# The opening of a two layer encoder: order of the input loads, of the first operands and of the first weight sums

## The chip, the cores and the metric

The kernel runs on one core of a Trainium2 chip. The metric is device time in microseconds (us) of one execution; a lower time is better. Five engines work beside each other, each through its own queue: TensorE (PE, matmuls; PEld are its weight loads), VectorE (DVE), ScalarE (ACT), GpSimd (POOL) and SyncE (SP). DMA transfers are issued from the queues of SP, ACT and POOL. All arithmetic is on float32 data; for matmuls each operand is split into a rounded part and a remainder, as told below.

## The reference

The program is a trunk of two macaron layers over 512 tokens plus 16 learned meta tokens, 528 in all, of width 1024. Each layer is a half-weighted SwiGLU block, a mixer of two parallel branches (gated linear attention and grouped-query softmax attention), and another half-weighted SwiGLU block:

```python
def swiglu(x, w_gate, w_up, w_down):
    return (jax.nn.silu(x @ w_gate) * (x @ w_up)) @ w_down

def reference(x, meta_tokens, norm_gains, ...):
    h = jnp.concatenate([meta, x], axis=1)
    for l in range(DEPTH):
        h = h + 0.5 * swiglu(rmsnorm(h, norm_gains[l, 0]), ffn_w_gate[l, 0], ffn_w_up[l, 0], ffn_w_down[l, 0])
        h = h + mixer(rmsnorm(h, norm_gains[l, 1]), ...)
        h = h + 0.5 * swiglu(rmsnorm(h, norm_gains[l, 2]), ffn_w_gate[l, 1], ffn_w_up[l, 1], ffn_w_down[l, 1])
    return rmsnorm(h, final_norm)[:, N_META:]
```

Only the first SwiGLU block of layer 0 is touched by the change: `rmsnorm`, then `x @ w_gate` and `x @ w_up` with an inner width of 2816.

## The kernel before

**Layout.** The tokens lie along the free dimension. `h` (`hall`) is one tile of 128 partitions x 8 chunks x 528 tokens; chunk c holds features 128c to 128c+127. `halves` are the token ranges 0:264 and 264:528, `HF` is 264.

**Two parts for each operand.** A value is used as `hi`, its copy rounded to the matmul type by ACT, and `lo`, value minus `hi`, by DVE. A product is three matmuls: hi x hi, hi x lo, lo x hi. For weights the two parts are made by `Weights.make` (cast on line 290 into `whi`, difference on line 291 into `wlo`), for 128x1024 at a time, in four buffers each.

**Seven products in place of eight.** The gate and up products of the SwiGLU block take the two by two block scheme with seven products (Strassen's, in a form with chained sums). The activations' blocks are two chunks (a pair j of chunks 2j and 2j+1) by two token halves: b11, b12 are the halves of the first chunk, b21, b22 those of the second. The weights' blocks 11, 12, 21, 22 are stored as 128x1024 pieces in `win`. Products are named "1" to "7". Each is 24 matmuls of 128x264: four chunk pairs k, gate and up (j), three combinations of parts. Products 1, 2 and 4 use the weight blocks 11, 12 and 22 as they are (`DIRECT`). Products 7, 6, 5 and 3 use sums of blocks: s3 = 21 - 11, s2 = 22 + s3, s1 = 21 + 22, s4 = s2 - 12. The activations' side has seven blocks for each pair, in the order of `PLACE`: b11 (product 1), b21 (product 2), b12 - b11 (5), b22 minus that (6), b12 - b22 (7), b21 minus the block of product 6 (4), and -b22 (3). `Norm.pair` (line 508) makes all seven, in both parts, from two chunks scaled by the norm's gain (line 512): casts on lines 519 and 524, differences on 520, 525, 527, 528, 530 and 531.

**Columns of weights.** The 2816 inner columns are 11 pairs of 128-wide column blocks for gate and up, in groups of 4, 4 and 3. "P0-1" in what follows is product 1 of column pair 0. `ffn_steps(True)` gives the first block the order P0-1, P0-2, P1-1, P1-2, P0-4, P1-4, P0-6, P0-5, P0-7, P0-3, P1-6, P1-5, P2-1, P1-7, P2-2, P1-3, P2-6, and so on. `product_of_pair` (line 584) runs one product; its results are collected in PSUM tiles X, Y, Z and W and in SBUF tiles `c` (copies on lines 605 and 615, adds on line 611, 626, 627, 634). When a column pair is complete, `hidden` applies silu and the gate (lines 651, 447, 661).

**Sums of weights.** For column pairs 0 to 3 of the first block the sums are made by accumulating DMAs of POOL (`add`, line 209): ACT writes the negative of block 11 or 12 (line 204), POOL adds further blocks onto it out of DRAM or out of SBUF. `begin_sums` makes s3 and s2, `first_sum` makes s1, and `sums` calls them when the parts of a product's weights are made: in the first block's column pairs 0 and 1 (`OPENING`) `begin_sums` at product 1, `first_sum` and s4 at product 2. The tiles of s3 and s4 share three buffers (`long`), those of s2 and s1 another three (`short`). POOL's adds stand in one queue, so an add that waits holds up those behind it.

**Loads.** `fetch` issues the weights' loads on SP in the order of use, into three buffers (`raw`); a buffer is free again when the cast, the difference and, where there is one, the negative of it have run. `use` makes the parts three products ahead and fetches nine loads ahead.

**The norm.** The sum of squares (`Norm.square`, lines 502 and 506) is begun ahead of P0-5. A matmul with a constant matrix (line 474) gives the means, and ACT and DVE the reciprocal root (lines 480, 447, 485, 486, 558). It is needed only in `hidden`, since the norm's factor is applied behind the products. Line 768 scales the chunks of h with it; these are traced among the steps of column pairs 2 and 3.

**What sets the order.** The text is traced into instructions with dependencies, and a planner then orders each engine's queue by the order of the text and by which instruction it believes ready; an instruction whose inputs or buffer it believes not ready is passed by later ones. `issue_after` and `W.behind` pin an instruction behind another of the same engine. On the chip each queue then runs strictly in that order.

**The opening.** SP loads chunk 0, chunk 1, the first weights in two pieces, then chunks 2 to 7 in three loads. `first.pair(j)` alternates with `W.make`:

```python
    nc.sync.dma_start(h(1), xt[:, 1])
    first.pair(0)
    W.fetch(1)
    for c in (2, 4, 6):
        nc.sync.dma_start(hall[:, c : c + 2], xt[:, c : c + 2])
    W.make(1)
    W.fetch(2)
    first.pair(1)
```

Of the kernel before, what the change touches and what calls it, by code (L numbers as in the profile page):

```python
# [17 lines left out]
P = 128  # L18
# [153 lines left out]
class Weights:  # L172
# [41 lines left out]
    def begin_sums(self, f, i, w=None):  # L214

        got = self.summed
        s3 = None
        if self.chained(f, i):
            s3 = self.negative(f, i, "s3", w)
            self.add(s3, self.dram(f, i, "21"))  # L220
        elif i < NPAIR:
            s3 = self.block(f, i, "21", self.long, "wsa")
        s2 = self.block(f, i, "22", self.short, "wsb")
        if self.chained(f, i):
            self.add(s2, s3)
        got[f, i, "7"], got[f, i, "6"] = s3, s2
        if (f, i) not in OPENING:
            self.first_sum(f, i)

    def first_sum(self, f, i):  # L230
        s1 = self.block(f, i, "21", self.short, "wsb")
# [100 lines left out]
def build(tc, ctx, xt, wts, win, par, w2, const, umask, out):  # L332
# [32 lines left out]
    def nm(p):  # L365
        count[0] += 1
        return f"{p}{count[0]}"
# [22 lines left out]
    def h(c, cs=None):  # L390
        return hall[:, c, cs or slice(0, live[0])]
# [4 lines left out]
    nc.sync.dma_start(h(0), xt[:, 0])  # L396
    S.dma_start(pt, par)
    def load_constants():
        S.dma_start(ct[:, :C_O1024], const[:, :C_O1024])
# [88 lines left out]
    class Norm:  # L488


        def __init__(self, gc):
            self.gc, self.x, self.acc = gc, [], None

        def operand(self, c):
            hi, lo = slot("x", F32R), slot("x", F32R)
# [12 lines left out]
        def pair(self, j):  # L508
# [23 lines left out]
            parts(slice(4, 6), v2(t34))  # L532
            self.x.append((hi, lo))

        def chunk(self, c):
            self.operand(c)
            self.square(c)
# [35 lines left out]

    pending = [load_constants]

    def ffn(l, f, norm, done, following):

        x, rs, up, n = norm.x, None, None, live[0]
        w = n // 2
# [177 lines left out]
        for i, step in enumerate(steps):  # L757
# [26 lines left out]

    def project(x, rs, tag, f=1.0, n=T):
# [445 lines left out]
    def ending(sums, operand, rs):  # L1231
# [49 lines left out]
    nc.sync.dma_start(h(1), xt[:, 1])  # L1281
    first.pair(0)
# [6 lines left out]
    W.make(2)  # L1289
    W.fetch(3)  # L1290
    first.pair(2)
    W.make(3)
    W.fetch(4)
    first.pair(3)
    nc.sync.dma_start(ct[:, C_O1024 : C_O1024 + P], const[:, C_O1024 : C_O1024 + P])

    norms = [first] + [Norm(G_NORM + i * KC) for i in range(1, 3 * DEPTH)]
    for l in range(DEPTH):
        a, b, c = norms[3 * l : 3 * l + 3]
        ffn(l, 0, a, b.chunk, lambda: operand_pools(b, "x"))  # L1300
# [79 lines left out]
```

## Time and profile before

| | us |
|---|---|
| median of 3 runs (lowest, highest) | 2196.23 (2196.23, 2197.56) |
| the profiled execution's own time | 2196.04 |
| its span in the profile | 2194.3 |
| DVE busy | 1777.9 |
| ACT busy | 1215.5 |

In the profile "L601" is line 601 of the kernel, "out<-in" gives the tiles written and read, "x24" a count, and what stands in brackets is the idle time of the engine just before the instruction and what ended it. Times count from the start of the span. `ss<-xc,whi` is a matmul with the rounded weights, `ss<-xc,wlo` one with their remainder, `w<-win` a load of a weight block, or an add onto one, and `s` a tile of s3 or s4. The same bytes of DMA are read in both kernels: 16.78 MB in the first 60 us here.

### The profile page before, as it was taken

The numbers are of one execution on the slowest core, as the hardware profiler recorded it, in microseconds if no ns is written. First come the engines' busy times: TensorE is split into PE (matmuls) and PEld (weight loads), VectorE is DVE, ScalarE is ACT, GpSimd is POOL, SyncE is SP. The second block draws the span as 40 slices with busy tenths as digits, with TensorE's granted clock in tenths as the row PEclk, the third lists the DMA queues.
The fourth block names the chain that finished last, engine by engine and source line by source line (L and its number), as shares of the span: only waits on it lengthen the run. The fifth ranks groups of instructions, "written<-read, shape, count | busy, mean of one in ns | idle before, by whom it ended". The sixth has DMA issues, their size and how long they took to land.

```text
span 2194.3 us, 40087 instructions
## 1 busy us (share of the span) xinstructions
PE 2157.0 (98%) x16506; PEld 2066.7 (94%) x16506; DVE 1777.9 (81%) x2699; ACT 1215.5 (55%) x1781; POOL 105.3 (5%) x124
## 2 busy tenths in 40 slices
PE   7999999999999999999999999999999999999998
PEld 7999999989999999999999999999788888999997
DVE  7887977586976689788799879785878767997987
ACT  8545545354784556454575455453557836554543
POOL 1100000000000000010010000000000001000100
PEclk9999999999999999999999999999999999999999
DMA  9866743212113567676667667432121145776752
GB/s 282 218 194 184 200 125 111 78 49 68 49 39 120 129 176 182 202 182 184 165 164 186 198 181 203 127 109 80 49 78 49 49 134 151 197 202 181 195 161 68
DMA packets 87751, 312.46 MB, mean 142 GB/s; under 512 B 9744, under 2 KB 12176, under 8 KB 87568
## 3 DMA queue, kind: packets, MB, share of 16 engines
q1 hardware_dynamic: 68336, 244.48, 33.6%
q0 software_dynamic: 17280, 62.92, 16.1%
q10 hardware_dynamic: 1952, 2.50, 0.4%
q8 instruction: 130, 2.13, 0.4%
q14 instruction: 53, 0.43, 0.1%
HBM read 289.94 MB, written 2.10 MB: 133 GB/s over the span
## 4 chain that ended last, share of the span: by engine, by line
PE 76%; DVE 16%; ACT 4%; issue 2%; DMA 2%; SPq 0%; POOL 0%; DVEq 0%; ACTq 0%
PE ss L601 33%; PE mm L468 13%; PE ss L721 11%; PE ss L468 10%; DVE wlo L291 4%; PE sm L468 2%; DVE g L687 1%; PE sm L1083 1%; DVE c L683 1%; DVE g L683 1%; PE ss L1058 1%; DVE c L651 1%; DMA w<-win 1%; DVE g L661 1%; PE ss L474 1%
## 5 line engine op out<-in xcount | busy, mean ns | idle before, releaser
L601 PE MATMUL ss<-xc,whi 128*128 128x264 f32 (+1 forms) x4928 | 903.4, 285 | 11.6 <-ACT whi L290 7.4
L601 PEld LDWEIGHTS ss<-xc,whi 128*128 128x128 f32 x4928 | 764.8, 189 | 14.9 <-ACT whi L290 7.8
L601 PE MATMUL ss<-xc,wlo 128*128 128x264 f32 (+1 forms) x2464 | 700.7, 285 | 3.4 <-DVE wlo L291 3.3
L601 PEld LDWEIGHTS ss<-xc,wlo 128*128 128x128 f32 x2464 | 465.1, 189 | 5.2 <-DVE wlo L291 5.2
L291 DVE TENSOR_TENSOR wlo<-w,whi 128x1024 fp32r<-128x1024 f32 (+1 forms) x335 | 405.5, 1217 | 64.1 <-ACT whi L290 63.9
L290 ACT CAST whi<-w 128x1024 fp32r<-128x1024 f32 (+1 forms) x335 | 345.9, 1048 | 159.8 <-PE ss L601 80.3
L468 PE MATMUL mm<-x,whi 128*128 128x264 f32 (+1 forms) x1712 | 384.8, 315 | 0.0
L468 PEld LDWEIGHTS mm<-x,whi 128*128 128x128 f32 x1712 | 278.4, 188 | 16.6 <-issue 1.0
L468 PE MATMUL mm<-x,wlo 128*128 128x264 f32 (+1 forms) x856 | 266.1, 315 | 0.0
L721 PE MATMUL ss<-g,whi 128*128 128x264 f32 (+1 forms) x1280 | 237.0, 284 | 0.0
L290 ACT CAST whi<-raw 128x1024 fp32r<-128x1024 f32 x126 | 132.1, 1049 | 163.5 <-PE mm L468 102.7
L605 ACT COPY c<-ss 128x528 f32<-128x528 f32 (+1 forms) x132 | 78.5, 595 | 245.7 <-PE ss L601 245.3
L291 DVE TENSOR_TENSOR wlo<-raw,whi 128x1024 fp32r<-128x1024 f32 x126 | 153.9, 1222 | 59.3 <-ACT whi L290 58.4
L721 PEld LDWEIGHTS ss<-g,whi 128*128 128x128 f32 x1280 | 198.4, 188 | 0.1
L721 PE MATMUL ss<-g,wlo 128*128 128x264 f32 (+1 forms) x640 | 181.3, 283 | 0.0
L468 PEld LDWEIGHTS mm<-x,wlo 128*128 128x128 f32 x856 | 159.6, 188 | 8.5 <-issue 0.7
L468 PE MATMUL ss<-g,whi 128*128 128x264 f32 (+2 forms) x900 | 166.2, 299 | 0.0
L468 PEld LDWEIGHTS ss<-g,whi 128*128 128x128 f32 x900 | 131.7, 188 | 5.2
L209 POOL DMA_DIRECT2D w<-win x60 | 52.7, 879 | 1557.1 <-DVE t L1211 392.2
L721 PEld LDWEIGHTS ss<-g,wlo 128*128 128x128 f32 x640 | 120.5, 188 | 0.0
L447 ACT ACTIVATE c<-c 128x528 f32<-128x528 f32 (+1 forms) x88 | 56.5, 642 | 96.3 <-DVE c L651 96.1
L291 DVE TENSOR_TENSOR wlo<-s,whi 128x1024 fp32r<-128x1024 f32 x86 | 104.9, 1220 | 1.7 <-ACT whi L290 1.5
(268 smaller groups left out, 3374.0 us busy)
## 6 DMA issues: line engine op xcount, KB each, us to landing
w<-win SPq DMA_DIRECT2D x333, 512.0 KB, 4.5
raw<-wts SPq DMA_DIRECT2D x126, 512.0 KB, 3.3
w<-win POOLq DMA_DIRECT2D x60, 512.0 KB, 7.4
s<-win POOLq DMA_DIRECT2D x26, 512.0 KB, 7.6
w<-s POOLq DMA_DIRECT2D x26, 512.0 KB, 6.0
s<-w POOLq DMA_DIRECT2D x8, 512.0 KB, 8.0
h<-xt SPq DMA_DIRECT2D x3, 528.0 KB, 6.6
out<-h ACTq DMA_DIRECT2D x4, 256.0 KB, 2.4
```

Of the source, the lines that this page charges most:

```text
L209: self.nc.gpsimd.dma_start(t, src, accum_op=ALU.add)
L290: nc.scalar.copy(hi[:, cs], w[:, cs])
L291: nc.vector.tensor_tensor(lo[:, cs], w[:, cs], hi[:, cs].bitcast(F32), ALU.subtract)
L447: prev_act[0] = S.activation(*args, **kw).ins
L468: TE.matmul(acc.half[i][:width], lhs, rhs[:, acc.spans[i]], start=first, stop=last)
L474: TE.matmul(a, weights, x[:, hs], start=True, stop=True)
L601: TE.matmul(acc[:, j], a[:, j, k], b[:, at], start=bool(begin and k == 0 and i == 0), stop=k == len(x) - 1 and i == 2, skip_group_check=no ...
L605: W.behind = S.copy(part(st, q), acc).ins
L651: V.scalar_tensor_tensor(td, ts, -0.5, rs[:, cs], ALU.mult, ALU.mult)
L661: V.tensor_tensor(raw[p // 4][2 * m + q][:, p % 4], t[:, q * w : (q + 1) * w], us, ALU.mult)
L683: V.tensor_tensor(lo, src[:, ks], hi.bitcast(F32), ALU.subtract)
L721: TE.matmul(acc[:, j], a[:, j, k], xs[b][:, k], start=bool(begin and k == 0 and i == 0), stop=k == 3 and i == 2, skip_group_check=not begin)
```

## The change

The edits are all in the first block of layer 0.

1. The loads of x go by token halves: first halves of chunks 0 and 1, P0-1's weights, first halves of chunks 2 and 3, then of 4 to 7, the weights of P0-2 and P1-1, then the second halves.
2. `Norm.pair` isn't used for this block. `head` makes the operands of products 1 and 2 (b11 and b21) straight from `h`, for all four pairs, ahead of the products. `fourth` scales whole chunks and makes the operand of product 4, `middle` those of 5 and 6, `rest` those of 7 and 3. They are called between the steps of `ffn`: `fourth` for pairs 0 and 1 behind P0-1, for 2 and 3 behind P0-2, `middle` for all behind P1-2, `rest` behind P0-4.
3. For column pairs 0 and 1 the negatives are written at products 1 and 2 as before; the loads and adds of the sums (`open_sums`) stand behind P0-2 for pair 0 and behind P1-2 for pair 1.
4. `warm_up(9)` puts nine float32 matmuls on a zeroed tile ahead of everything on PE. Their result isn't used.

```diff
+        self.first_sum(f, i)
+
+    def open_sums(self, f, i):
+
+        got = self.summed
+        self.add(got[f, i, "7"], self.dram(f, i, "21"))
+        s2 = got[f, i, "6"] = self.block(f, i, "22", self.short, "wsb")
+        self.add(s2, got[f, i, "7"])
+        self.first_sum(f, i)
+        self.add(got[f, i, "3"], s2)
...
-        if (f, i) in OPENING and product in "12":
-            (self.begin_sums if product == "1" else self.first_sum)(f, i, *[w] * (product == "1"))
-        if i < 2:
+        if (f, i) in OPENING:
+            if product in "12":
+                name, into = ("s3", "7") if product == "1" else ("s4", "3")
+                got[f, i, into] = self.negative(f, i, name, w)
+        elif i < 2:
...
-    nc.sync.dma_start(h(0), xt[:, 0])
+    nc.sync.dma_start(hall[:, 0:2, :HF], xt[:, 0:2, :HF])
...
+    def warm_up(n):
+        z = slot("rs")
+        V.memset(z, 0.0)
+        into = pair()
+        for i in range(n):
+            TE.matmul(into[:, i % 2, :HF], z[:, :P], z[:, P : P + HF], start=True, stop=True)
...
+        def head(self, j):
+
+            hi, lo = self.tiles()
+            for i in range(2):
+                src, g = h(2 * j + i, slice(0, live[0] // 2)), col(self.gc + 2 * j + i)
+                scaled_in = S.activation(hi[:, i], src, AF.Identity, scale=g).ins
+                V.scalar_tensor_tensor(lo[:, i], src, g, hi[:, i].bitcast(F32), ALU.mult, ALU.subtract)
+            return scaled_in
+
+        def fourth(self, j):
+
+            w = live[0] // 2
+            raw, t = twin("g"), twin("g").rearrange("p a (b c) -> p (a b) c", b=2)
+            for i in range(2):
+                S.activation(raw[:, i], h(2 * j + i), AF.Identity, scale=col(self.gc + 2 * j + i))
+            b11, b12, b21, b22 = [raw[:, i, a : a + w] for i in range(2) for a in (0, w)]
+            V.tensor_tensor(t[:, 0], b12, b11, ALU.subtract)
+            V.tensor_tensor(t[:, 1], b22, t[:, 0], ALU.subtract)
+            V.tensor_tensor(t[:, 3], b21, t[:, 1], ALU.subtract)
+            self.parts(j, 5, t[:, 3])
+            self.left.append((t, b12, b22))
+
+        def middle(self, j):
+            self.parts(j, slice(2, 4), self.left[j][0][:, 0:2])
+
+        def rest(self, j):
+            (hi, lo), (t, b12, b22) = self.x[j], self.left[j]
+            V.tensor_tensor(t[:, 2], b12, b22, ALU.subtract)
+            self.parts(j, 4, t[:, 2])
+            S.activation(hi[:, 6], b22, AF.Copy, scale=-1.0)
+            V.scalar_tensor_tensor(lo[:, 6], b22, -1.0, hi[:, 6].bitcast(F32), ALU.mult, ALU.subtract)
...
+            for call in between.get(i, ()):
+                call()
...
+    warm_up(9)
     first = Norm(G_NORM)
...
+    def load_x(c, n, cs):
+        nc.sync.dma_start(hall[:, c : c + n, cs], xt[:, c : c + n, cs])
+
     W.fetch(1)
-    for c in (2, 4, 6):
-        nc.sync.dma_start(hall[:, c : c + 2], xt[:, c : c + 2])
+    load_x(2, 2, halves[0])
+    load_x(4, 4, halves[0])
+    W.fetch(2)
+    W.fetch(3)
+    load_x(0, 4, halves[1])
+    load_x(4, 4, halves[1])
+    W.behind = first.head(0)
     W.make(1)
-    W.fetch(2)
-    first.pair(1)
...
+    W.behind = None
+    for j in range(1, KC // 2):
+        first.head(j)
...
+    begin = [lambda i=i: W.open_sums((0, 0), i) for i in range(2)]
+    between = {0: each(first.fourth, range(2)), 1: each(first.fourth, range(2, 4)) + begin[:1], 3: begin[1:] + each(first.middle),
+               4: each(first.rest)}
```

More of the change, by code (lines that the diff above doesn't have):

```diff
@@ L491, in __init__ @@
         def __init__(self, gc):
[L492 removed]
+            self.gc, self.x, self.acc, self.left = gc, [], None, []
         def operand(self, c):
@@ L574, in build, with ffn @@
     pending = [load_constants]
-    def ffn(l, f, norm, done, following):
+    def ffn(l, f, norm, done, following, between={}):
         x, rs, up, n = norm.x, None, None, live[0]
@@ L1280, in build, with each @@
     bp = [block_pools()]
-    nc.sync.dma_start(h(1), xt[:, 1])
-    first.pair(0)
+    def load_x(c, n, cs):
+        nc.sync.dma_start(hall[:, c : c + n, cs], xt[:, c : c + n, cs])
     W.fetch(1)
-    for c in (2, 4, 6):
-        nc.sync.dma_start(hall[:, c : c + 2], xt[:, c : c + 2])
-    W.make(1)
-    W.fetch(2)
-    first.pair(1)
[L1289 to L1294, printed above, removed]
-    nc.sync.dma_start(ct[:, C_O1024 : C_O1024 + P], const[:, C_O1024 : C_O1024 + P])
+    load_x(2, 2, halves[0])
[5 more added lines that the diff above has]
+    W.behind = first.head(0)
+    W.make(1)
+    W.behind = None
+    for j in range(1, KC // 2):
+        first.head(j)
+    nc.sync.dma_start(ct[:, C_O1024 : C_O1024 + P], const[:, C_O1024 : C_O1024 + P])
+    def each(stage, js=range(KC // 2)):
+        return [lambda j=j: stage(j) for j in js]
+    begin = [lambda i=i: W.open_sums((0, 0), i) for i in range(2)]
+    between = {0: each(first.fourth, range(2)), 1: each(first.fourth, range(2, 4)) + begin[:1], 3: begin[1:] + each(first.middle),
+               4: each(first.rest)}
     norms = [first] + [Norm(G_NORM + i * KC) for i in range(1, 3 * DEPTH)]
@@ L1299, in build @@
         a, b, c = norms[3 * l : 3 * l + 3]
-        ffn(l, 0, a, b.chunk, lambda: operand_pools(b, "x"))
+        ffn(l, 0, a, b.chunk, lambda: operand_pools(b, "x"), between if l == 0 else {})
         close_pools(bp.pop())
```

11 lines of the change are left out of this document (9 added, 2 removed).

## The prediction

> **What bounds the kernel now.** I read the page's busy shares first, then stretches of the opening, then TensorE's timeline there, then the queues that feed it.
>
> ```profile
> span 2194.3 us, 40087 instructions
> PE 2157.0 (98%) x16506; PEld 2066.7 (94%) x16506; DVE 1777.9 (81%) x2699; ACT 1215.5 (55%) x1781; POOL 105.3 (5%) x124
> ```
>
> TensorE (PE) is busy 98% of the span: 2194.3 - 2157.0 = 37 us are all that a better order can win, besides a slow clock. The stretches show where they lie (columns: busy time of PE, weight load, DVE, ACT, POOL; clock; DMA share; GB/s).
>
> ```profile
> 0.00:7.41 7.41, 0.00 (x1) 0.01 (x1) 2.50 (x8) 4.68 (x9) 0.20 (x4) 1.00 0.77 247
> 7.41:18.97 11.56, 8.89 (x30) 7.14 (x31) 11.21 (x24) 10.46 (x20) 1.01 (x1) 1.00 1.03 354
> 18.97:39.00 20.03, 18.53 (x142) 17.46 (x141) 16.82 (x24) 18.48 (x29) 4.42 (x5) 1.00 1.05 293
> 41.22:50.00 8.78, 8.78 (x72) 8.75 (x71) 6.30 (x9) 6.49 (x8) 1.79 (x2) 1.00 1.00 207
> 50.00:64.70 14.70, 14.63 (x120) 14.42 (x119) 14.21 (x21) 9.21 (x11) 2.62 (x3) 1.00 1.00 256
> ```
>
> From 41.22 PE runs without a gap: 72 matmuls in 8.78 us, 0.122 us each, so a product of 24 matmuls takes 2.93 us. Write P0-1 for pair 0's product 1. The opening order is P0-1, P0-2, P1-1, P1-2, P0-4, P1-4, P0-6, then P0-5, P0-7, P0-3. Seven products are worth 7 x 2.93 = 20.5 us, and they are done at 39.0: 18.5 us are lost, plus 1.4 us ahead of the norm's matmuls (below). In the same stretches DVE and ACT work 11.21 and 10.46 of 11.56 us, then 16.82 and 18.48 of 20.03: the two engines that make the operands are nearly full too. That is the main limit on what can be won.
>
> ```profile
> 7.41 0.81 PE L601 MATMUL ss<-xc,whi 128*128 128x264 f32 x2 [7.41 <-ACT whi L290]
> 18.75 0.42 PE L601 MATMUL ss<-xc,wlo 128*128 128x264 f32 x1
> 18.97 0.51 PE L601 MATMUL ss<-xc,whi 128*128 128x264 f32 x2
> 25.63 0.51 PE L601 MATMUL ss<-xc,whi 128*128 128x264 f32 x2
> 26.89 0.39 PE L601 MATMUL ss<-xc,wlo 128*128 128x264 f32 x1 [0.75 <-DVE wlo L291]
> 40.44 1.13 PE L474 MATMUL ss<-t,const 128*128 128x264 f32 x4 [1.45 <-ACT whi L290]
> 41.22 0.59 PE L601 MATMUL ss<-xc,whi 128*128 128x264 f32 x2
> ```
>
> The start costs 7.41 us. Until 18.97 starts lie 0.22 us apart (18.75 to 18.97) against 0.122 later: 30 matmuls at 0.10 us too much, 2.9 us. The rest are waits. P1-2 starts at 25.63, so three products are done then, and it ends at 29.6.
>
> **The change, part by part.**
>
> *Loads.* Each issue of SyncE's queue below is followed by its time to landing (median, of one):
>
> ```profile
> 0.74 0.39 SPq L396 DMA_DIRECT2D h<-xt  x1
> h<-xt SPq DMA_DIRECT2D x1, 264.0 KB, 3.0
> 5.91 0.55 SPq L199 DMA_DIRECT2D w<-win  x1
> w<-win SPq DMA_DIRECT2D x1, 512.0 KB, 12.9
> 9.46 0.33 SPq L199 DMA_DIRECT2D w<-win  x1
> w<-win SPq DMA_DIRECT2D x1, 512.0 KB, 11.9
> 28.62 0.33 SPq L199 DMA_DIRECT2D w<-win  x1
> 32.87 1.46 SPq L199 DMA_DIRECT2D w<-win  x2
> ```
>
> The first half chunk, issued at 0.74, lands at 3.7. P1-1's weights (5.91) land at 18.8 behind 4.3 MB, P1-2's (9.46) at 21.4. In the new order P1-1 has 2.1 MB ahead. From 3.7 on, at the 354 GB/s of the stretch to 18.97, the halves of P0-1's weights land at 4.4 and 5.2, first halves of x at 5.9 and 7.4, P0-2's weights at 8.9, P1-1's at 10.4, second halves of x at 11.9 and 13.4. That the pieces of x are rows of 1,056 B instead of 2,112 I price at nothing (bounds: 0 and, were these 2.1 MB twice as slow, 6 us for the last of them but 1.5 us for the first half pair).
>
> *Head instead of the whole pair.* Each of four pairs needs two ACT and two DVE instructions before the first four products:
>
> ```profile
> 4.01 1.36 ACT L512 ACTIVATE t<-h,par 128x528 f32<-128x528 f32 x2 [1.99 <-DMA par<-par]
> 5.89 0.42 ACT L524 ACTIVATE xc<-t 128x264 fp32r<-128x264 f32 x1
> 6.22 0.61 ACT L519 CAST xc<-t 128x528 fp32r<-128x528 f32 x1
> 6.74 1.13 ACT L290 CAST whi<-w 128x512 fp32r<-128x512 f32 x2
> 39.17 1.05 ACT L290 CAST whi<-s 128x1024 fp32r<-128x1024 f32 x1
> 40.26 1.22 DVE L291 TENSOR_TENSOR wlo<-s,whi 128x1024 fp32r<-128x1024 f32 x1
> ```
>
> Starts give the true pace: 0.33 us for a half (5.89 to 6.22), 0.53 for 528, 0.64 for L512, 0.96 for a weight cast, 1.14 for its DVE part. With parameters at 4.0, head 0 ends at 4.7, P0-1's cast at 6.1 and its difference on DVE at 6.8, then a negative, and heads 1 to 3 by 9.5. P0-2's cast and difference end at 11.4, P1-1's (a negative between) at 13.3: P0-2 ends at 14.1, P1-1 at 17.0, eight us ahead of 25.6.
>
> *Nine matmuls on zeros.* The fp32 pair of L474 takes 41.22 - 40.44 = 0.78 us, 0.39 each; nine are 3.5 us at the fast clock, 6.3 at 1.8 times that. From about 1.4 (a memset of at most 0.7 us by the nearest 528 wide DVE work) they end between 4.9 and 7.7. P0-1 can't finish its first six matmuls before 6.8, so I price the delay at nothing, at most 0.9. What they remove is the slow pitch, 2.9 us at most, already in the times above. [...]
>
> *Fourth product, middle, rest, sums.* These move behind products 1 to 4. No work vanishes:
>
> ```profile
> L502 ACT ACTIVATE t<-h 128x528 f32<-128x528 f32 x8 | 4.7, 634 | 0.0
> L204 ACT ACTIVATE s<-w 128x1024 f32<-128x1024 f32 x4 | 4.2, 1052 | 0.0
> L605 ACT COPY c<-ss 128x528 f32<-128x528 f32 x3 | 1.8, 591 | 0.3 <-PE ss L601 0.3
> L615 ACT COPY c<-ss 128x528 f32<-128x528 f32 x2 | 1.2, 582 | 0.0
> ```
>
> These are the norm's squares, the negatives and the copies of PSUM in the first 41 us; from start to start each is some 0.09 shorter. ACT has per pair 2 x 0.34 + 2 x 0.63 + 0.33 + 0.53 + 2 x 0.33, in all 13.8 us against 13.3; DVE about 0.3 us more. Up to P0-3's weight cast ACT must do those 13.8, the casts 1.0 + 9 x 0.96, four negatives 3.8, five copies 2.5 and eight squares 4.4: 34.1 us. From 4.0, with 1.0 of idle time while the first halves land, this ends at 39.1; with the 1.5 us more that waits may add, 40.6 (before: 40.2). DVE follows 1.2 later. So P0-3 can end at 40.3 + 22 x 0.122 = 43.0 to 44.5, and with the norm's 0.8 at 43.8 to 45.3. Before it ended at 50.0. **The lead is 4.7 to 6.2 us; I take 5.5.** The 8 us of P1-1 are not kept, because the ACT stays full: PE only eats the lag that it had behind ACT.
>
> *Sums' loads and adds.* The chain by GpSimd:
>
> ```profile
> 9.17 1.01 POOL L209 DMA_DIRECT2D s<-win  x1 [8.72 <-ACT s L204]
> 19.01 0.87 POOL L209 DMA_DIRECT2D w<-s  x1 [8.83 <-DMA s<-win]
> 39.63 0.86 POOL L209 DMA_DIRECT2D w<-win  x1 [2.07 <-DVE t L506]
> 47.98 2.00 ACT L290 CAST whi<-w 128x1024 fp32r<-128x1024 f32 x2 [0.30 <-DMA w<-win]
> ```
>
> The add at 39.63 lands about 48, and P1-5's cast at 47.98 waits for it; PE takes P1-5 at 52.9. With a cast and a difference P1-5's weights are ready at 50.1: 2.8 us of slack, and a PE that is 5.5 us early needs them 2.7 us sooner. Its first add waits only for the negative of P0-1's weights, which now comes at about 7.2 instead of 9.1; behind it the queue is bound by DMA time. That makes 0.8 us short; since the buffers that the later links wait for come free earlier too, I take 0.5 us lost (bounds: 0, and 2.7 if nothing of the chain comes sooner). Queued behind a waiting add is every later add of POOL.
>
> The profiled execution took 2196.04 (span 2194.3, 1.7 around it; the median of the runs is 2196.23). 2196.0 - 5.5 + 0.5 = **2191.0 us**; own range 2188 (lead 8, if nothing of ACT's lag is met) to 2193.
>
> **Rivals.**
>
> *VectorE eats the lead.*
>
> ```profile
> 43.70 0.71 DVE L485 SCALAR_TENSOR_TENSOR t<-ss,t 128x528 f32<-128x528 f32 x1 [2.23 <-ACT t L447]
> 46.94 1.32 DVE L768 SCALAR_TENSOR_TENSOR h<-h,rs 128x528 f32<-128x528 f32 x2
> 56.26 2.56 DVE L768 SCALAR_TENSOR_TENSOR h<-h,rs 128x528 f32<-128x528 f32 x4
> 60.04 1.22 DVE L291 TENSOR_TENSOR wlo<-w,whi 128x1024 fp32r<-128x1024 f32 x1
> ```
>
> From 43.7 to 62 DVE has no pause, and P2-2's difference (60.04 to 61.26) comes 0.4 us ahead of its product at 61.7. With second halves of x late, DVE idles some 3 us more before 15. If the reciprocal root then still starts at 43.7, P2-2 holds PE to a lead near 1: 2195. Against it: six or more of the 0.64 us L768 can slip behind that difference. It decides where the norm's sum comes no earlier than 40.3.
>
> *The sums come late: slower.* If POOL's first add is issued where the text now puts it, behind the second product (about 15 instead of 9.2), six us pass down the chain: 39.63 becomes 45.6, P1-5's weights are ready at 56 on DVE against 52.9, and the next pair's, which need the same three buffers, are as late again: 2196 + 3.1 + 3.1 = 2202. It decides from a first add after some 12.5. For it: the text; against it: an add ready on an idle POOL was issued at once at 9.17.
>
> *The loads don't move.* Queues run what is ready, not the text's order: the loads at 28.62 (a buffer freed by a weight at 28.6) pass P1's sum, which waits until 32.87. The sums' blocks need nothing, so SyncE may issue them right behind x, ahead of P1-2. Then P1-2's weights land at 21 as before, and it ends at 21 + 0.96 + 1.14 + 22 x 0.122 = 25.8 instead of about 20 to 22; against 29.6 that is a lead of 3.8, the ACT work behind it comes in at that lead, and 2192.2 results.
>
> *The clock falls back.* The first two products come in bursts between 7 and 12. If that shuts the clock again, 2.9 us return: 2193.9. The pauses that I expect there are under 1.5 us; in the trace the clock stays fast over the 1.45 ahead of 40.44. [...]
>
> **How the numbers follow.** Forecast 0.53, VectorE 0.15, late sums 0.20, loads unmoved 0.10, clock 0.02. Within 0.2% is about what a measurement of this kernel can tell from no change: 4.4 us. Faster than 2191.8: nearly all of the forecast (0.51) and a third of "unmoved", 0.54; slower than 2200.6: most of the late sums, 0.18; the rest 0.28. The range is 2188 to 2200: the lower bound of the lead, and up to where late sums alone are left.
>
> **What would show it.** Right: a fast pitch from the first product on; P1-1 done before 19 us; ten products and the norm done by 45; P1-5's cast not waiting for a DMA. Wrong: SyncE issuing three sums' blocks ahead of P1-2's (unmoved); POOL's first add after 12 (late sums); DVE's norm sum at 40 or later and PE waiting on differences near 60 (VectorE); a 0.22 pitch after 8 us (clock). A PE lead at 50 us that isn't the change of the span would mean a loss behind the opening that I haven't priced.

## The result, and the profile after

The changed kernel takes 2200.14 us (median of 16 runs, 2198.91 to 2203.13), the kernel before 2196.82 beside it (16 runs, 2194.79 to 2198.51): a ratio of 1.0019, interval 1.0012 to 1.0025. That is 3.3 us slower, where 5.2 us faster was forecast (2191.0 against 2196.23). The profiled execution took 2200.14, its span is 2198.4, 4.1 us more than before. Times here and below are medians; one of seven runs of the kernel "after, zeros in the gap" took 2597.24 us, and its median is that of the other six.

The same stretches of the changed kernel from 7.41 us on (busy time of PE, weight load, DVE, ACT, POOL; clock; DMA share; GB/s):

```profile
7.41:18.97 11.56, 10.07 (x71) 8.85 (x70) 8.59 (x17) 10.79 (x17) 1.87 (x2) 1.00 1.05 351
18.97:39.00 20.03, 14.41 (x95) 13.53 (x96) 15.75 (x30) 14.94 (x29) 3.49 (x4) 0.91 1.03 275
39.00:41.22 2.22, 1.77 (x15) 1.56 (x14) 1.70 (x4) 1.80 (x4) 0.00 (x0) 1.00 0.05 9
41.22:50.00 8.78, 6.45 (x45) 5.59 (x44) 7.32 (x10) 6.96 (x11) 2.65 (x3) 0.94 0.95 244
```

The third of these in the kernel before:

```profile
39.00:41.22 2.22, 0.78 (x5) 0.71 (x5) 2.12 (x3) 1.22 (x2) 0.86 (x1) 1.00 1.12 207
```

From 7.41 to 18.97 PE does 71 matmuls where it did 30. Then it does 95 instead of 142, and from 41.22 on 45 instead of 72. In the second stretch ACT, which had been nearly full there, is busy for 14.94 of 20.03 us instead of 18.48, and DVE for 15.75 instead of 16.82. In the third the DMA engines move 9 GB/s, where they moved 207.

How far PE is can be counted. These are the groups of product matmuls up to 30 and up to 60 us, first of the kernel before, then of the changed one (busy time, mean ns, idle before):

```profile
L601 PE MATMUL ss<-xc,whi 128*128 128x264 f32 x66 | 16.5, 344 | 9.3 <-ACT whi L290 7.4 <-ACT xc L519 1.6 <-DVE xc L520 0.2
L601 PE MATMUL ss<-xc,wlo 128*128 128x264 f32 x33 | 11.3, 343 | 2.3 <-DVE wlo L291 2.3
...
L601 PE MATMUL ss<-xc,whi 128*128 128x264 f32 x214 | 43.9, 304 | 9.3 <-ACT whi L290 7.4 <-ACT xc L519 1.6 <-DVE xc L520 0.2
L601 PE MATMUL ss<-xc,wlo 128*128 128x264 f32 x107 | 32.5, 304 | 2.4 <-DVE wlo L291 2.3
```

```profile
L661 PE MATMUL ss<-xc,whi 128*128 128x264 f32 x95 | 18.8, 295 | 0.9 <-ACT whi L300 0.5 <-ACT xc L568 0.3
L661 PE MATMUL ss<-xc,wlo 128*128 128x264 f32 x47 | 13.6, 293 | 2.3 <-DVE wlo L301 2.2
...
L661 PE MATMUL ss<-xc,whi 128*128 128x264 f32 x193 | 39.8, 304 | 4.6 <-ACT whi L300 3.7 <-ACT c L665 0.4 <-ACT xc L568 0.3
L661 PE MATMUL ss<-xc,wlo 128*128 128x264 f32 x96 | 28.8, 304 | 3.1 <-DVE wlo L301 2.9
```

66 + 33 = 99 against 95 + 47 = 142: at 30 us the changed kernel is 43 matmuls, 5.2 us at 0.122, ahead. At 60 it is 321 against 289: 32 matmuls, 3.9 us, behind. Beyond that the distance hardly moves (36 matmuls at 100 us). So nearly all is decided between 30 and 60, and the table below counts every kernel in this way. PE's timeline there:

```profile
6.91 0.60 PE L661 MATMUL ss<-xc,whi 128*128 128x264 f32 x2
...
18.44 0.28 PE L661 MATMUL ss<-xc,wlo 128*128 128x264 f32 x1
...
33.64 0.51 PE L661 MATMUL ss<-xc,whi 128*128 128x264 f32 x2 [3.17 <-ACT whi L300]
34.90 0.40 PE L661 MATMUL ss<-xc,wlo 128*128 128x264 f32 x1 [0.75 <-DVE wlo L301]
...
35.66 0.65 PE L661 MATMUL ss<-xc,whi 128*128 128x264 f32 x2
36.10 0.42 PE L661 MATMUL ss<-xc,wlo 128*128 128x264 f32 x1
36.32 0.65 PE L661 MATMUL ss<-xc,whi 128*128 128x264 f32 x2
...
48.16 1.35 PE L491 MATMUL ss<-t,const 128*128 128x264 f32 x4 [2.22 <-issue]
```

Before, P0-6 (the matmuls from the 145th on) started without a wait:

```profile
35.54 0.41 PE L601 MATMUL ss<-xc,whi 128*128 128x264 f32 x2
```

In the changed kernel PE is done with six products at 30.5 us, and P0-6 starts at 33.64 after a wait of 3.17 us, with another of 0.75 for its remainder. Behind it three matmuls take 0.66 us (35.66 to 36.32), 0.22 each: the granted clock is 0.50 from 35.27 to 38.68. The norm's means stand at 48.16, before at 40.44, and 2.22 us of idle time precede them. P0-3, the tenth product, ends at 53.8, before at 49.9.

What P0-6 waits for stands on ACT, and behind that on POOL and SP:

```profile
32.54 1.04 ACT L300 CAST whi<-w 128x1024 fp32r<-128x1024 f32 x1 [5.06 <-DMA w<-s]
...
39.91 2.78 ACT L519 ACTIVATE t<-h 128x528 f32<-128x528 f32 x5
```

```profile
8.48 1.00 POOL L209 DMA_DIRECT2D s<-win  x1 [8.03 <-ACT s L204]
...
25.47 0.86 POOL L209 DMA_DIRECT2D w<-s  x1 [9.92 <-DMA w<-win]
...
32.81 0.86 POOL L209 DMA_DIRECT2D s<-w  x1 [3.86 <-DMA w<-s]
```

```profile
15.12 0.93 SPq L199 DMA_DIRECT2D w<-win  x2
...
w<-win SPq DMA_DIRECT2D x2, 512.0 KB, 10.2
...
SPq L199 <- DMA s<-w: 23.4, 2, 13.9
```

The add that makes P0-6's sum (w<-s) is issued at 25.47, where it was at 19.01. It had waited for a plain block: SyncE issued it at 15.12, the first of the two in the row above, behind P1-2's, P0-4's and P1-4's, and it landed 9.8 us later at 24.9 (10.2 is the median of the two). The other tile of this add, s3, had landed at 17.1. ACT sat 5.06 us at that cast, and the squares, which stand behind it on that queue, ran at 39.91. The add into s4 (32.81) followed, and SyncE's next sum's block waited up to 13.9 us for the buffer that this add reads.

### The profile page after: what moved, and what is told of

Read it like the earlier page. It is cut to its first block, busy times and chain, and to the rows that moved or that the text cites. A ratio compares the mean times of both kernels' runs of the same rounds, so it can differ in the third digit from the quotient of the medians.

```text
span 2198.4 us, 40135 instructions
## 1 busy us (share of the span) xinstructions
PE 2162.5 (98%) x16524; PEld 2071.0 (94%) x16524; DVE 1778.8 (81%) x2704; ACT 1216.1 (55%) x1785; POOL 105.0 (5%) x124
## 4 chain that ended last, share of the span: by engine, by line
PE 76%; DVE 16%; ACT 4%; issue 2%; DMA 1%; SPq 0%; DVEq 0%; ACTq 0%; POOLq 0%
PE ss L661 33%; PE mm L485 13%; PE ss L781 11%; PE ss L485 10%; DVE wlo L301 4%; PE sm L485 2%; DVE g L747 1%; PE sm L1145 1%; DVE c L743 1%; DVE g L743 1%; DVE c L711 1%; PE ss L1120 1%; DVE g L721 1%; PE ss L491 1%; DVE h L789 1%
## 5 line engine op out<-in xcount | busy, mean ns | idle before, releaser
L661 PEld LDWEIGHTS ss<-xc,whi 128*128 128x128 f32 x4928 | 764.5, 189 | 10.2 <-ACT whi L300 4.1
L485 PE MATMUL ss<-g,wlo 128*128 128x264 f32 (+2 forms) x450 | 106.3, 300 | 0.0
```

Source lines behind the costliest of these rows:

```text
L485: TE.matmul(acc.half[i][:width], lhs, rhs[:, acc.spans[i]], start=first, stop=last)
L661: TE.matmul(acc[:, j], a[:, j, k], b[:, at], start=bool(begin and k == 0 and i == 0), stop=k == len(x) - 1 and i == 2, skip_group_check=no ...
```

## The experiments

Each kernel ran beside the kernel before on the same chip. The table gives the ratio with its interval and the count of product matmuls up to a time. The times are medians of 11 runs, of 16 in the first two rows, of 5 in "sums as before" and of 6 in "zeros in the gap" and "after, fourth buffer".

| kernel | us | ratio | at 30 | at 38 | at 48 | at 60 | at 100 |
|---|---|---|---|---|---|---|---|
| before | 2196.82 | | 99 | 165 | 225 | 321 | 645 |
| after | 2200.14 | 1.0019 (1.0012 to 1.0025) | 142 | 161 | 216 | 289 | 609 |
| before, zeros | 2197.23 | 1.0001 (0.9992 to 1.0010) | 99 | 162 | 205 | 303 | 629 |
| after, no zeros | 2201.85 | 1.0020 (1.0011 to 1.0029) | 143 | 159 | 216 | 284 | 600 |
| before, sums moved | 2199.57 | 1.0013 (1.0004 to 1.0021) | 104 | 169 | 225 | 323 | 647 |
| after, sums as before | 2205.13 | 1.0032 (1.0019 to 1.0044) | 73 | 121 | 201 | 250 | 577 |
| after, block early | 2202.33 | 1.0024 (1.0015 to 1.0033) | 119 | 168 | 216 | 271 | 592 |
| after, zeros in the gap | 2203.31 | 1.0026 (1.0015 to 1.0037) | 141 | 167 | 210 | 261 | 588 |
| after, squares early | 2201.94 | 1.0020 (1.0011 to 1.0029) | 141 | 164 | 222 | 312 | 606 |
| after, POOL's order | 2200.80 | 1.0017 (1.0008 to 1.0026) | 139 | 169 | 216 | 287 | 605 |
| after, fourth buffer | 2203.42 | 1.0032 (1.0021 to 1.0044) | 134 | 158 | 216 | 282 | 594 |
| before, fourth buffer | 2201.67 | 1.0022 (1.0013 to 1.0031) | 95 | 161 | 223 | 321 | 610 |
| after, adds on DVE | 2201.04 | 1.0020 (1.0011 to 1.0029) | 137 | 158 | 216 | 281 | 601 |
| before, adds on DVE | 2197.49 | 1.0004 (0.9995 to 1.0013) | 86 | 151 | 219 | 316 | 642 |
| after, no adds | 2194.04 | 0.9987 (0.9978 to 0.9996) | 149 | 208 | 242 | 337 | 648 |
| before, no adds | 2195.09 | 0.9991 (0.9982 to 0.9999) | 109 | 171 | 243 | 342 | 650 |
| after, no adds, squares early | 2193.88 | 0.9986 (0.9977 to 0.9995) | 144 | 171 | 237 | 333 | 648 |
| after, sums in order | 2201.63 | 1.0021 (1.0012 to 1.0030) | 129 | 189 | 229 | 316 | 593 |
| the same, squares early | 2199.47 | 1.0013 (1.0004 to 1.0022) | 129 | 161 | 224 | 316 | 601 |
| the same, adds on DVE | 2198.49 | 1.0008 (0.9999 to 1.0017) | 131 | 164 | 213 | 309 | 619 |

(A count is that of the one profiled execution; the one of "before, zeros" took 2199.03, over its median.)

### The zeros

Before, with only the zeros, and after, without them:

```diff
+    warm_up(9)
     first = Norm(G_NORM)
```

> The kernel before, with the nine products on zeros ahead of its first product and nothing else of the change. Both theories: in the kernel before the first products follow the loads (VectorE's and ScalarE's casts and the blocks' landings set PE's gaps up to 20 us), so the zeros at best give the first product a fast pitch, which the next gap takes away. Theory A (the change lost its time at the sums' late blocks): 2197 +- 1.2, no change. Rival (the pitch of the first products is on the path that sets the end): 2195.0 to 2196.0, the two to four slow products' time gained.

> The changed kernel without the nine matmuls on zeros. Theory A: products 1 to 4 run at the slow pitch (0.22 us) for some 4 us longer and end 2 to 3 us later, but the block that lands at 25.4 and its add at 32.5 are where they were, so P0-6 starts at 33 to 34 as now; time within 1 us of 2200. Rival C (the zeros delay the start and cost time): first product at 5 to 6 us, time 2198 or less. Rival D (the zeros are what the change wins, and all of it reaches the end): 2202 or more.

Before with zeros: 1.0001; after without them: 1.0020 against 1.0019 with them. They cost and bring nothing that can be measured. Without them the first product started at 5.51 and P0-6 at 33.73 again.

### The place of the sums' loads, alone and undone

```diff
-            (self.begin_sums if product == "1" else self.first_sum)(f, i, *[w] * (product == "1"))
+            got[f, i, into] = self.negative(f, i, name, w)
...
+    between = {1: begin[:1], 3: begin[1:]}
```

> The kernel before, with only the sums' loads and adds placed as in the changed kernel (each pair's block for its sum issued behind the plain blocks of products 2 and 1-2, and not ahead of them). Theory A (a sum is late only where its product comes early; the block lands when its buffer and the queue let it): in the kernel before product 0-6 is wanted at 35.6 us, so a sum that is done at 32 to 34 us still comes in time, and the blocks of P1-1 and P1-2 land sooner by the transfers taken from ahead of them: 2195 to 2198. Rival B (the sums' blocks in the changed kernel's place are late whatever the rest does, and the place costs the whole loss): 2199 to 2202, with a gap on PE ahead of P0-6 that a DMA ends.

> The changed kernel with the weight sums' loads and adds where they were before (input halves, split operands and nine matmuls kept). The two blocks of pair 0 come ahead of P1-2's weights again. Theory A: P1-2 starts some 2 us later than in the changed kernel (21 instead of 19.2), but no gap of over 1 us before P0-6, means by 43, time 2190 to 2194. Theory B: means at 46 or later, 2198.5 to 2201.5.

Moving the sums in the kernel before costs 2.6 us (1.0013), but the profile of its fastest execution shows no gap ahead of P0-6 and counts within five of those before up to 100 us: where its other executions lose it stays open. (The three slowest of them have a mean granted clock of 0.996, the others 0.997 to 0.999.) Undoing the move in the changed kernel is no better than the change (1.0032 from five runs; the intervals overlap): the sums' blocks then stand ahead of P1-2's, whose product waits 11.64 us at 29.64. By the counts at 60 us (289 against 250) the new place is the better one for this opening, and it is still late for P0-6.

### One link at a time

The block of P0-6's sum issued right behind x:

```diff
     load_x(4, 4, halves[1])
+    W.early[0, "22"] = W.block((0, 0), 0, "22", W.short, "wsb")
     W.behind = first.head(0)
```

> The changed kernel with one load moved: the plain load of P0-6's weight sum (block 22) is issued right behind the second halves of x, instead of behind P1-4's weights. Theory A (the late block: issued at 15.1, landed at 25.4, added to until 32.5, ACT stuck behind it for 5.1 us): the block lands by 18, its add starts at 17 to 18, P0-6's cast starts by 27, PE's gap of 3.2 us before P0-6 falls under 1 us, no slow pitch after 10 us, the norm's means by 43; time 2190 to 2193. Theory B (the operand work moved between the products makes ACT and DVE late whatever the loads do): means still at 46 or later, time within 1.5 us of 2200.

It missed (1.0024). PE's timeline of that kernel:

```profile
21.51 0.51 PE L662 MATMUL ss<-xc,whi 128*128 128x264 f32 x2 [3.47 <-ACT whi L301]
...
34.18 0.40 PE L662 MATMUL ss<-xc,whi 128*128 128x264 f32 x2
34.76 0.39 PE L662 MATMUL ss<-xc,wlo 128*128 128x264 f32 x1 [0.17 <-DVE wlo L302]
...
39.58 0.50 PE L662 MATMUL ss<-xc,whi 128*128 128x264 f32 x2 [1.88 <-ACT whi L301]
...
49.61 0.68 PE L492 MATMUL ss<-t,const 128*128 128x264 f32 x1 [2.89 <-issue]
```

P0-6's wait is gone but for 0.17 us, yet it starts at 34.18, no sooner than in the change (33.64): P1-2, whose block the early one pushed back, waits 3.47 us and makes the products behind it late. P0-5 then waits 1.88, and the means come at 49.61.

Nine matmuls that add zeros, put into the gap ahead of P0-6 to keep the clock up:

```diff
+            if (l, f, p, product) == (0, 0, 0, "6"):
+                with tc.issue_after(last_mm[0]):
+                    for i in range(9):
+                        TE.matmul(acc[:, i % 2], zero[0][:, :P], zero[0][:, P : P + w], start=False, stop=False, skip_group_check=True)
```

> The changed kernel with nine more matmuls on zeros held between P1-4 and P0-6 (they add zero to the sums). They fill some 3.5 us, the gap is about 3.2 + 0.75. If the clock alone is the loss (rival E): the 18 slow matmuls after the gap go fast, PE is 1.8 us earlier for good, time 2198.3 or less. Theory A: the pitch after the gap stays fast, but the norm's means still wait for the squares that stand behind P0-6's cast in ACT's queue (48.2), so PE waits longer there and the end moves by less than 1 us: 2199 to 2201.

1.0026, though the granted clock stayed at 1.00 from 27 to 43 us: the clock behind P0-6's wait alone is not the loss. The means came at 48.09 and a product behind them waited 2.70 us.

The eight squares ahead of P0-6's cast, GpSimd's second s3 held back, a fourth buffer for sums (paid for with one of the six buffers of the `t` pool), and the first pair's adds on VectorE:

```diff
-    3: begin[1:] + each(first.middle),
+    3: begin[1:] + each(first.middle) + each(first.square, range(KC)),
```

```diff
+        with self.tc.issue_after(self.last) if self.last else nullcontext():
             self.add(got[f, i, "7"], self.dram(f, i, "21"))
```

```diff
-        pools = open_pools("left", wsa=3, wsb=3)
+        pools = open_pools("left", wsa=3, wsb=short)
...
-dict(g=8, t=6, rs=2)
+dict(g=8, t=5, rs=2)
```

```diff
                 w = self.summed.pop(load)
+                if load == ((0, 0), 0, "6"):
+                    nc.vector.tensor_tensor(w, w, self.summed[(0, 0), 0, "7"], ALU.add)
...
+            elif (f, i) == OPENING[0]:
+                V.tensor_tensor(got[f, i, "3"], got[f, i, "3"], w, ALU.add)
```

> The changed kernel, with the first norm's eight squares (ScalarE) called ahead of product 0-6's cast and not behind product 0-5's. ScalarE takes its work in order and sits 5.06 us at that cast until the sum has landed; the squares fill that wait. Theory A (the late sum costs twice: once at P0-6 itself, 3.17 us, and once more through ScalarE's queue, by the norm's means at 48.2 us with a 2.22 us wait and 2.6 us of slow pitch behind it): means by 42 to 45 us, no gap of PE ahead of them above 1 us, 2196.0 to 2198.0. Rival B (the norm isn't what the end waits for: the weights' transfers are): the means come sooner, but the gap goes to the next cast, 2199.5 to 2201.

> The changed kernel, with the accumulating load of the second pair's s3 held behind the add that makes product 0-6's sum, as it stood on GpSimd's queue in the kernel before (there at 26.55 us; in the changed kernel it passed ahead, at 14.68 us). Theory A' (that load takes its share of the DMA engines from P0-4, P1-4 and the block of P0-6's sum): these land 1 to 1.5 us sooner, P0-6's cast starts at 31 to 31.6 and not 32.5, 2198.0 to 2199.5. Rival (the queue is held by buffers, not by the share): P0-6's cast stays at 32.0 or later and the second pair's sums come later, 2200 to 2203.

> The changed kernel, with a fourth buffer for the sums' blocks in the first block (and five instead of six buffers of the t pool, to make room). Theory D, formed after the last runs: SyncE issues its loads in order, and from 26.11 to 40.48 us it stood at the load of the second pair's s1, whose buffer is free only when the add into s4 of the first pair has read it (issued 32.81 us behind P0-6's late sum, landed 40.4); the DMA engines ran empty (138 and 4 GB/s in the two slices from 36 to 41 us by the kernel page's slices of the first 75 us), and the blocks behind it on that queue came 3.5 to 7 us late, which the end waits for. With one buffer more that load needs no wait on that add: SyncE's wait on an add falls from 23.4 us to under 13 us, no stretch of 2 us is below 150 GB/s between 30 and 45 us, P0-6's own wait stays (2.5 to 4 us): 2197.0 to 2199.3. Rival E (the price is P0-6's wait and the clock that falls back behind it, whatever the queue does): 2199.5 to 2202.

> The kernel before with the same fourth buffer (and five t buffers). It too has a wait of SyncE of 12.2 us on an add, at a time when the blocks ahead are already there. Theory D: 2195 to 2197.2 (that wait ends at 32.87 us there, ahead of PE's need). Rival E: 2196.5 to 2198, no change.

> The changed kernel, with the first pair's two adds from SBUF to SBUF (s3 into s2, then s2 into s4) made by VectorE at P0-6's cast and behind it, in place of two accumulating transfers of 7.0 and 7.6 us on GpSimd's queue. Theory D (the chain of dependent transfers behind one late block is the loss, at P0-6 and at SyncE's next buffer): P0-6's cast at 26.5 to 28.5 us, PE's wait there under 1.2 us, the second pair's s1 issued by 34 us, 2193.5 to 2197.5, the forecast's lead kept in part. Rival B (the lead is bounded by what the DMA engines can bring, and the next block is late in its turn, as in the run with the early block): 2198.5 to 2201 with another DMA wait of 2 us or more on the way to 66 us.

> The kernel before with the same two adds on VectorE. Theory D and B alike: the sum isn't what PE waits for there (products run without a gap from 27 to 39 us), so little: 2195 to 2197.5; slower, to 2199, if VectorE's add stands ahead of other work while its block is on the way, since VectorE is the busiest engine up to 40 us.

None is faster than the change: 1.0020, 1.0017, 1.0032 and 1.0020. With the squares early the norm left the path, as theory A had it, and PE was level with the kernel before at 52 us (255 matmuls each); yet the time stayed. In that kernel PE shows:

```profile
39.30 1.05 PE L491 MATMUL ss<-t,const 128*128 128x264 f32 x4
```

The means at 39.30 wait for nothing; but at 60.39, 61.33 and 63.19 PE waits 0.53 and 0.44 us for casts and 1.35 for a remainder, 2.3 us within 3, and the clock is 0.50 from 62.95 to 66.36. With GpSimd's order P0-6's cast came sooner (its wait 0.95 us) and a later product waited 2.06. With the fourth buffer SyncE still waited 25.4 us in all for such adds, up to 13.6 at one load. Nor did it serve the kernel before, which became 5 us slower (1.0022); whether by the buffer gained or by the `t` buffer given up for it, no run tells. With the adds on VectorE P0-6 waited 1.43 us and P0-5, whose own sum was late, 2.39. Theories A and D, in which one link carries the loss, fell.

### Without the sums' transfers

If the sums are the whole loss, a kernel that leaves them out must keep the lead. Both kernels, without the eight accumulating transfers of the first two pairs, and the changed one with the squares early as well:

```diff
+        if self.whole:
             self.nc.gpsimd.dma_start(t, src, accum_op=ALU.add)
```

> The changed kernel, with the first two pairs' eight accumulating transfers left out (their sums are the plain blocks or negatives alone, so these pairs' products are computed from incomplete operands). Theory F (the lead is lost to sums that come late, several in a row, and nothing else): PE runs on through P0-6 and P0-5 without a wait over 1 us, the count of matmuls at 60 us is 30 to 45 above the same leaving-out made in the kernel before, and the time is 3.5 to 5.5 us below that one: 2189 to 2193. Rival G (the norm, the casts and the operands behind the fourth product hold PE at 40 to 50 us whatever the sums do): within 1.5 us of that one, 2194 to 2198.

> The kernel before, with the same eight transfers left out. Both theories: the sums aren't what PE waits for there up to 60 us, but the transfers left out free the DMA engines for the blocks of P1-1, P1-2 and the third pair: 2193 to 2197.

> The changed kernel without the first two pairs' eight adds (operands incomplete, as before) and with the eight squares ahead of P0-6's cast. Theory F' (two holders in a row: the sums, and behind them the norm whose squares stand behind P0-5's cast on ScalarE): the norm's means by 37 to 39 us, the lead of 30 matmuls and more over the kernel before without the adds is there at 60 us (342 + 30), and the time is 2190.0 to 2192.0, 3 to 5 us under that kernel's 2195.1. Rival G' (the transfers or the casts hold it next, whatever the norm does): 2193 to 2195.

2194.04 against 2195.09, with overlapping intervals (and overlapping runs: up to 2194.50 against 2193.67 and more): rival G's number. Groups up to 38 us, of after and then of before, both without the adds:

```profile
L665 PE MATMUL ss<-xc,whi 128*128 128x264 f32 x139 | 26.5, 289 | 0.5 <-ACT c L669 0.5
L665 PE MATMUL ss<-xc,wlo 128*128 128x264 f32 x69 | 19.7, 291 | 2.5 <-DVE wlo L305 2.4
```

```profile
L605 PE MATMUL ss<-xc,whi 128*128 128x264 f32 x114 | 25.1, 318 | 9.3 <-ACT whi L294 7.4 <-ACT xc L523 1.6 <-DVE xc L524 0.2
L605 PE MATMUL ss<-xc,wlo 128*128 128x264 f32 x57 | 18.1, 318 | 1.6 <-DVE wlo L295 1.6
```

208 against 171: the lead, 37 matmuls or 4.5 us, is there at 38 us, so the sums' transfers were what took it first. (Leaving them out takes away their lateness and their traffic together; the pair does not tell the two apart.) At 48 us the lead is gone (242 against 243). ACT, DVE and PE of the changed kernel without adds show how:

```profile
33.18 2.79 ACT L523 ACTIVATE t<-h 128x528 f32<-128x528 f32 x5
...
36.81 1.71 ACT L523 ACTIVATE t<-h 128x528 f32<-128x528 f32 x3
38.41 1.05 ACT L304 CAST whi<-s 128x1024 fp32r<-128x1024 f32 x1
```

```profile
39.90 1.22 DVE L305 TENSOR_TENSOR wlo<-s,whi 128x1024 fp32r<-128x1024 f32 x1
41.03 0.70 DVE L527 TENSOR_TENSOR t<-t,t 128x528 f32<-128x528 f32 x1
```

```profile
41.84 1.13 PE L495 MATMUL ss<-t,const 128*128 128x264 f32 x4 [2.61 <-issue]
43.31 0.65 PE L665 MATMUL ss<-xc,whi 128*128 128x264 f32 x2 [0.34 <-DVE c L691]
```

From 28.7 to 39.9 us ACT runs without a pause, and reaches P0-3's cast at 38.41. PE has used up what was prepared: its ninth product ends at 39.2, and it stands 2.61 us until the last of the squares' sums is made, which follows P0-3's difference on DVE and ends at 41.73. P0-3 starts behind the means, at 43.31, and the clock is 0.50 from 43.45 to 46.86: P0-3 ends at 47.8, in the kernel before without adds at 47.6. Putting the squares first only moves this. In that kernel PE waited at P0-6 and P0-5:

```profile
31.38 0.51 PE L665 MATMUL ss<-xc,whi 128*128 128x264 f32 x2 [1.62 <-ACT whi L304]
32.94 0.39 PE L665 MATMUL ss<-xc,wlo 128*128 128x264 f32 x1 [1.04 <-DVE wlo L305]
39.30 0.39 PE L665 MATMUL ss<-xc,wlo 128*128 128x264 f32 x1 [0.98 <-DVE wlo L305]
```

and its stretches (columns as above) have both operand engines full, with the DMA engines nearly idle from 30 to 40:

```profile
20.00:30.00 10.00, 8.98 (x70) 8.54 (x70) 10.00 (x21) 10.00 (x19) 0.00 (x0) 1.00 0.57 196
30.00:35.00 5.00, 2.57 (x18) 2.36 (x19) 4.83 (x9) 5.00 (x13) 0.00 (x0) 1.00 0.21 59
35.00:40.00 5.00, 3.72 (x21) 2.66 (x20) 5.00 (x10) 4.97 (x8) 0.00 (x0) 1.00 0.12 48
```

ACT 19.97 and DVE 19.83 of 20 us, at a DMA share of 0.57 down to 0.12: here the lead of 35 matmuls at 30 us is eaten by 38 (171 against 171), and neither engine waits for a transfer in that time.

### The adds in place, and all links together

The two blocks issued between the plain ones and GpSimd's adds in the order of need; then the squares early as well; then the first pair's two adds on VectorE too:

```diff
+    for upto, name in ((4, "22"), (5, "21")):
+        W.fetch(upto)
+        W.early[0, name] = W.block((0, 0), 0, name, W.short, "wsb")
```

> The changed kernel, with the first pair's two blocks for sums issued between the plain blocks (behind P1-2's and behind P0-4's, not behind P1-4's), and GpSimd's adds in the order s3, s2, s1 of the first pair before any of the second. Theory F: both sums by 30 to 33 us, P0-6's wait under 1.5 us and P0-5's under 1.5 us, 2196.5 to 2199.5. Rival B (the DMA engines are full from 10 to 30 us at a share above 1.0, so what is brought sooner makes another block late by as much): waits at P1-2, P0-4 or P1-4 of 2 us and more, or at the second pair's sums, 2199.5 to 2203.

> As the last, with the squares ahead of P0-6's cast as well. Theory F: both links mended, the norm's means by 43 us, count at 60 us 320 or more: 2194 to 2198. Rival B: 2199 to 2203.

> The changed kernel with the blocks and GpSimd's adds of the first pair in order, the squares early, and the first pair's two adds from SBUF to SBUF made by VectorE. Theory B' (with the adds in place the transfers are the third holder: the run before it stood 2.73 us at a product near 69 us, with the DMA engines' share at 0.94 to 1.05 from 40 to 65 us): two transfers less, so that wait falls to under 1.5 us, 2195.5 to 2198.5. Rival (VectorE's two adds delay its own casts by their 2 x 1.2 us or stand waiting for a landing): 2199 to 2201.5.

1.0021, 1.0013, 1.0008. In the first P0-6 and P0-5 wait for no cast, at most 0.50 us for a remainder, as theory F had it, and it holds a lead of 24 matmuls at 38 us; then PE stands 2.43 us ahead of the means at 43.98. The first two are only five short of before at 60. They lose again behind it (52 and 44 short at 100), where a cast waits for a sum; in the second:

```profile
66.55 1.04 ACT L303 CAST whi<-w 128x1024 fp32r<-128x1024 f32 x1 [1.97 <-DMA w<-s]
```

The third is told apart neither from the kernel before nor from the second. In it PE waits 2.31 us for P0-4's remainder at 25.83, since one of VectorE's two adds (21.21 to 22.43) now stands ahead of it on that engine, as the rival had it. No version with whole sums beat the kernel before.

## Why the prediction was wrong

**Right.** The first four products came nearly as forecast: P0-1 at 6.91 at the fast pitch, P1-1 done by 18.7 (17.0 worked out, 25.6 before), P1-2's load at 8.27 and not behind the sums' blocks, so that "the loads don't move" was excluded. That the zeros open the clock ahead of the first product, on which the forecast's fast pitch there rests, was the author's estimate, and no run shows the time that they need for it; in the changed kernel the granted clock is 1.00 from 4.55 to 35.27, and three matmuls of P0-1 take 0.36 us (9.49 to 9.85), where three took 0.66 before (15.12 to 15.78). In the time the zeros cost nothing, and brought nothing.

**The sums, priced at 0.5 us (bounds 0 and 2.7).** This term failed. Its size can be taken from the pair without adds: with the adds the change costs 3.3 us, without them it brings 1.05, so they cost the change 4.4 us (lateness and traffic together). The step asked when GpSimd's first add is issued and followed one later add at 39.63; the first add did come sooner (8.48). It did not ask when the plain block of the second add is issued. That block passed from 4.03 us to 15.12, behind three weights' loads that wait for buffers, and the add slipped from 19.01 to 25.47 while P0-6 was due 5 us sooner (six products, 144 matmuls, were done at 30.5 us, before at 35.5). The rival "the sums come late" had the sign and nearly the size (2202), but its deciding point, the first add after 12.5 us, was the wrong place to look.

**The lead of 4.7 to 6.2 us, taken as 5.5.** This term failed too. The lead was there (5.2 us at 30 us), but would not have lasted: without the adds the change is worth 1.05 us, not told from none by the two kernels' intervals. So the sum that was forecast, 5.5 won and 0.5 lost, reads 1.05 won and 4.4 lost. The ACT sum of this step was good: P0-3's cast was forecast to end between 39.1 and 40.6, and in the kernel without adds it ends at 39.46, its difference at 41.12. What failed is the step from there, "P0-3 can end at 40.3 + 22 x 0.122 = 43.0 to 44.5, and with the norm's 0.8 at 43.8 to 45.3": P0-3 ended at 47.8. The step lets PE meet that difference with only 22 matmuls left, at the fast pitch, and counts the norm's means as 0.8 us of work and no wait. On PE the means stood ahead of P0-3, and they waited 2.61 us for the squares' sums on DVE; all of P0-3 came behind them, most of it at half the clock. P0-3's cast had ended at 40.2 before; ACT's work therefore ends only about a microsecond sooner, and what PE gains ahead is only the queue of prepared products that it had in front of it. That queue had hidden the norm's wait, the copies and the remainders. "VectorE eats the lead" was the nearest rival in kind, and near in size without the adds (a lead near 1). Its sign, a norm's sum on VectorE at 40 or later, was there: 41.03 without the adds, 47.36 with them. It put the place at P2-2 near 60 us, and the runs put it at P0-6 to P0-3 and the norm.

**"The clock falls back"** was looked for in the bursts up to 12 us, and happened behind the waits of 3.17 and 2.22 us; keeping it up behind the first by matmuls on zeros did not help.

**A reading.** The seven products before were done at 38.5 us, not at 39.0, by when PE had done 172 matmuls, four more than seven products; the forecast's sum does not use that time.

**Open.** With the adds' transfers in place each mended link was followed by another (P1-2, P0-5, the means, casts near 60 and 68 us), by different causes; which of them a full order of loads would leave last was not settled, nor how much of the 4.4 us is the sums' lateness and how much their traffic, nor why moving the sums in the kernel before costs 2.6 us in its other executions.

## What to carry to other kernels

In this opening a lead in the first products was worth only what the engine that makes operands gained at the last of them: compare the end of its own queue before and after, since a backlog in front of the bottleneck engine is also what hides later waits. When a load is moved, follow each dependent transfer to the product that needs it, and check the queue it now stands on. When several links are late together, mending one may not show in the time, as here; leave all of one kind out to see what lies behind.

## What the runs showed of the hardware

The granted clock of the changed kernel fell twice in the opening (columns as above), and the second fall followed a single wait of 2.22 us:

```profile
35.27:38.68 3.41, 3.41 (x18) 3.41 (x17) 3.41 (x8) 3.41 (x8) 0.00 (x0) 0.50 1.07 214
45.51:48.92 3.41, 1.19 (x8) 0.90 (x6) 2.99 (x5) 2.22 (x3) 0.62 (x1) 1.00 0.98 184
```

It was 1.00 from 4.55 to 35.27, 0.50 to 38.68, 1.00 to 48.92 and 0.50 to 52.34. The first fall came behind the waits of 3.17 and 0.75 us at P0-6; in the 3.41 us ahead of the second PE was idle for 2.22. In the kernel with the block early a stretch as long had 1.77 us of idle time (most of the 1.88 ahead of 39.58), at a clock of 1.00, and three matmuls behind it still took 0.37 us (41.07 to 41.44):

```profile
36.07:39.48 3.41, 1.64 (x14) 1.43 (x12) 1.39 (x5) 0.99 (x2) 0.00 (x0) 1.00 1.06 244
```

In the kernel without adds and with early squares the clock was 1.00 over the waits of 1.62 and 1.04 us and behind them (30 to 35 and 35 to 40 us, above). From which idle time on the clock falls was not shown.

The accumulating transfers on GpSimd's queue took about twice as much of the DMA engines' time for a MB as the plain loads on SyncE's. Queues of the kernel before, its first 75 us (packets, MB, share of 16 engines' time):

```profile
q0 software_dynamic: 1871, 6.82, 48.1%
q1 hardware_dynamic: 3928, 12.88, 47.2%
```

48.1 / 6.82 = 7.1% a MB on the queue of the adds against 47.2 / 12.88 = 3.7% on the loads'. Whether the adding or the other kind of queue makes the difference, no run here shows.
